# Cutting the first 8 MB load of a streaming row-sum kernel into an even-partition and an odd-partition load

## The chip, the cores and the metric

The kernel runs on one core of a Trainium2 chip. The metric is the device time of one execution in microseconds. The core has separate engines that run side by side and meet only at semaphores: VectorE (DVE in the profile), ScalarE (ACT), GpSimd (POOL), TensorE (PE, unused here) and SyncE (SP), which issues the transfers. The transfers themselves are moved by 16 DMA engines, each of which works through its own queue of packets in order.

## The reference

The input is float32 of shape 32 x 512 x 1024, so 16,384 rows of 1,024 numbers, 67.1 MB. Each row is clamped at zero and summed:

```python
relu_x = np.maximum(x, 0)
return np.sum(relu_x, axis=-1).astype(np.float32)
```

The output is 16,384 sums, 64 KB. Nearly all of the traffic is reading the input once.

## The kernel before, in words

The chip's memory for tiles (SBUF) has 128 partitions. The kernel gives each partition 128 rows in all: 16 rows from the first 2,048 rows of the input (`xf`), and 112 rows from the rest (`xv`). It goes through them in blocks of `ROWS = 16` rows per partition, which is 128 x 64 KB = 8 MB. There are `NB = 7` full blocks, and an eighth one that comes in smaller loads at the end (8 rows, 4 rows, then four pieces cut out of the last 4 rows). In the first block, partition p takes rows 16p to 16p+15, so the whole block is one contiguous 8 MB of the input, 64 KB of it per partition.

Three buffers `io0` to `io2` of 8 MB take the blocks in turn. The loads are all issued by SyncE in program order, through `load` (line 97, the transfer at line 99). Each load has its own semaphore from `sems.loads`, and adds 16 to it once all of it has landed. The first three loads wait for nothing. From the fourth on, a load waits on SyncE until VectorE has finished with the buffer it overwrites (line 101).

ScalarE clamps a block in place (`clamp`, lines 115 to 124) and VectorE sums its rows (`total`, lines 126 to 131). The lists `TWO`, `ACT` and `DVE` (lines 14 to 16) say how the rows of a block are cut: the first three blocks are clamped by one instruction each, later ones by two. The last rows go singly, some clamped and summed by ScalarE alone (`act_row`), some by VectorE alone (`dve_row`). ScalarE's very first instruction is the load of its function table, and that one carries the wait for the first block (line 118); the first clamp follows it without a wait of its own.

The order on SyncE is the order of the calls. Nothing schedules it anew, with one exception: `open_without_barrier` (line 241) takes the first `EARLY` instructions of SyncE (line 24, one before the change) out of the body and puts them into the program's opening block, ahead of everything else that SyncE does there. So the first load is SyncE's first instruction, then comes a branch to the body, then the second and third loads.

At the end SyncE issues three small stores: the sums of the first block, nearly all other sums, and the last two columns.

Of the kernel before, what the change touches and what calls it, by code (L numbers as in the profile page):

```python
# [5 lines left out]
RELU = mybir.ActivationFunctionType.Relu  # L6
# [3 lines left out]
ROWS = 16  # L10
NBUF = 3
# [9 lines left out]
START_PIECE, END_PIECE = 280, 260  # L21
PIECES = [240, 244]

EARLY = 1


def kernel(tc: tile.TileContext, x: bass.AP, out: bass.AP):
    nc = tc.nc
    sems = Semaphores(tc)

    tc.close()
    tc.compile()
    nc.cur_bb = nc.bb_map[tc.start_bb_name]
    body = nc.cur_bb.bb.instructions
    ends = list(body)
    body.clear()
    n_stores = relu_sum(nc, sems, x, out)
    body.extend(ends)


    nc.cur_bb = nc.bb_map[tc.start_bb_name + "_end"]
    nc.cur_bb.bb.instructions.clear()
    nums = sorted(s.num for s in (*sems.loads, sems.act, sems.dve))
    cleared = range(nums[0], nums[-1] + 1)
    assert len(cleared) == len(nums)
    nc.sync.sem_clear(cleared)
    nc.sync.wait_ge(sems.stored, 16 * n_stores).then_inc(sems.stored, -16 * n_stores)
    open_without_barrier(tc, EARLY)

# [10 lines left out]
def relu_sum(nc, sems: Semaphores, x: bass.AP, out: bass.AP):  # L60
# [24 lines left out]
    def rows(m, n):  # L85
        if m < ROWS:
            return xf[:, m : m + n, :]
        return xv[:, m - ROWS : m - ROWS + n, :]
# [5 lines left out]

    n_load = n_act = n_dve = n_store = 0

    def load(dst, src, after=None):
        nonlocal n_load
        dma = nc.sync.dma_start(out=dst, in_=src)  # L99
        if after:  # L100
            dma.wait_op(sems.dve, after[1], "sem-ge")
        dma.then_inc(sems.loads[n_load], 16)
        n_load += 1
        return sems.loads[n_load - 1]
# [10 lines left out]
    def clamp(ap, loaded):  # L115
        nonlocal n_act
        if n_act == 0:
            nc.scalar.preload_act_table(RELU).wait_op(loaded, 16, "sem-ge")  # L118
            loaded = None
        i = nc.scalar.activation(out=ap, in_=ap, func=RELU)  # L120
        if loaded is not None:
            i.wait_op(loaded, 16, "sem-ge")
        i.then_inc(sems.act, 1)
        n_act += 1

    def total(ap, m, n):
        nonlocal n_dve
        nc.vector.tensor_reduce(  # L128
            out=res[:, m : m + n], in_=ap, axis=mybir.AxisListType.X, op=ADD
        ).wait_op(sems.act, n_act, "sem-ge").then_inc(sems.dve, 1)  # L130
        n_dve += 1

    def act_row(ap, accum_out, loaded):
        nonlocal n_act
        i = nc.scalar.activation(out=ap, in_=ap, func=RELU, accum_out=accum_out)  # L135
        if loaded is not None:
            i.wait_op(loaded, 16, "sem-ge")
        i.then_inc(sems.act, 1)
        n_act += 1

    def dve_row(ap, accum_out, loaded):
        nonlocal n_dve
        i = nc.vector.tensor_scalar(  # L143
            out=ap,
            in0=ap,
            scalar1=0.0,
            scalar2=None,
            op0=MAX,
            op1=ADD,
            accum_out=accum_out,  # L150
        )
        if loaded is not None:
            i.wait_op(loaded, 16, "sem-ge")
        i.then_inc(sems.dve, 1)
        n_dve += 1

    freed = []
    m = 0
    for j in range(NB):
        buf = bufs[j % NBUF]  # L160
        loaded = load(buf[:, :, :], rows(m, ROWS), j >= NBUF and freed[j - NBUF])
        c = 0
        act_waits = dve_waits = loaded
        for n in TWO[j]:
            clamp(buf[:, c : c + n, :], act_waits)
            total(buf[:, c : c + n, :], m + c, n)
            act_waits = None
            c += n
        for _ in range(ACT[j]):
            act_row(buf[:, c, :], res[:, m + c : m + c + 1], act_waits)  # L170
            act_waits = None
            c += 1
        for _ in range(DVE[j]):
            dve_row(buf[:, c, :], res[:, m + c : m + c + 1], dve_waits)
            dve_waits = None
            c += 1
        assert c == ROWS
        freed.append((n_act, n_dve))
        m += ROWS


    buf = bufs[NB % NBUF]
    c = 0
    for n in TAIL:
        loaded = load(
            buf[:, c : c + n, :], rows(m, n), None if c else freed[NB - NBUF]
        )
        for i in range(n):
            if i % 2 == 0 or (n == 8 and i == 7):
                act_row(buf[:, c, :], res[:, m : m + 1], loaded if i == 0 else None)  # L190
            else:
                dve_row(buf[:, c, :], res[:, m : m + 1], loaded if i == 1 else None)
            c += 1
            m += 1

    flat = buf[:, :, :].rearrange("p c d -> p (c d)")
    src = rows(m, 4).rearrange("p c d -> p (c d)")
# [4 lines left out]
    last, w = parts[-1], PIECES[-1]  # L202
    others = [last[:, w + i : w + i + 1] for i in range(extra)]
    loaded = load(flat[:, at : at + b], src[:, :b])
    act_row(buf[:, c, :], res[:, m : m + 1], loaded)
    sums_act = n_act
# [3 lines left out]
    loaded = load(flat[:, at + end : at + 4 * D], src[:, end:])  # L210
# [30 lines left out]
def open_without_barrier(tc: tile.TileContext, n_loads: int):  # L241

    SP = mybir.EngineType.SP
    blocks = tc.nc.main_func.blocks
    opening = blocks[0].instructions
    body = next(b for b in blocks if b.name == tc.start_bb_name).instructions
    for i in list(opening):
        if isinstance(i, (mybir.InstDrain, mybir.InstEventSemaphore)):  # L250
            opening.remove(i)
    loads = [i for i in body if i.engine == SP][:n_loads]
    for i in loads:
        assert isinstance(i, mybir.InstDMACopy)
        body.remove(i)
    at = next(n for n, i in enumerate(opening) if i.engine == SP)
    opening[at:at] = loads
# [30 lines left out]
```

## Time and profile before

| | us |
|---|---|
| median of 3 runs | 160.94 (160.88 to 161.14) |
| span of the profiled execution | 159.8 |
| the runs' median over that span | 1.1 |
| VectorE busy | 117.6 |
| ScalarE busy | 104.2 |
| GpSimd busy | 0.2 |

The span runs from the first to the last instruction that the profile records, and it begins with SyncE's first load. The time of a run covers also what lies around the span; the profile does not carry the profiled execution's own time as a run, so it is taken as the span and the 1.1 us by which the median stands over it. An engine's idle time is put down to what released it. "SPq" stands for SyncE's queue of transfers, and an issue there is only the time that SyncE needs to start a transfer, not the transfer. Besides the engine rows, the trace has one record per DMA packet; a packet of a full block is one partition's 64 KB.

### The profile page before, as it was taken

The page shows a single profiled execution, that of the slowest core. Times are in us where ns is not written, and L with a number is a line of the kernel's source. Part 1 is how long each engine was busy: PE and PEld are TensorE (multiplying, and loading weights), DVE is VectorE, ACT ScalarE, POOL GpSimd, SP SyncE. Part 2 cuts the span into 40 slices and gives each one's busy share as a digit, 9 for nine tenths or more (in the row PEclk, how much of TensorE's full clock was granted, in tenths as well). Part 3 has the DMA queues.
Part 4 walks back from the last instruction along what each step waited for, and adds up shares of the span by engine and source line. Part 5 has one row for each costly group of instructions (what it writes and reads, how often), then busy time and mean ns, then how long its engine had stood idle before and what let it go on. Part 6 is the DMA issues. An engine that isn't in the chain of part 4 may idle for free.

```text
span 159.8 us, 120 instructions
## 1 busy us (share of the span) xinstructions
DVE 117.6 (74%) x43; ACT 104.2 (65%) x50; POOL 0.2 (0%) x4
## 2 busy tenths in 40 slices
DVE  0000000006999799994999999999999999999986
ACT  0000049993699808996099951999329993499994
POOL 0000000000000000000000000000000000000000
DMA  8996996996996997999989969969969969898993
GB/s 279 508 508 279 525 508 279 525 492 295 525 492 295 525 459 328 525 394 394 525 361 426 525 295 492 525 262 525 508 279 525 508 279 525 377 410 385 425 416 102
DMA packets 2304, 67.18 MB, mean 420 GB/s; under 512 B 640, under 2 KB 896, under 8 KB 1024
## 3 DMA queue, kind: packets, MB, share of 16 engines
q1 hardware_dynamic: 2304, 67.18, 97.9%
HBM read 67.11 MB, written 0.07 MB: 420 GB/s over the span
## 4 chain that ended last, share of the span: by engine, by line
DMA 44%; DVE 33%; ACT 17%; another core or an unknown queue 3%; SPq 1%; issue 0%
DMA io<-in_x_dram 44%; DVE res L128 32%; ACT io L120 17%; SPq L99 1%; DVE io L143 0%; DVE piece L227 0%; DVE piece L143 0%
## 5 line engine op out<-in xcount | busy, mean ns | idle before, releaser
L128 DVE TENSOR_REDUCE res<-io 128x8 f32<-128x8192 f32 (+2 forms) x9 | 101.1, 11286 | 40.2 <-ACT io L120 40.2
L120 ACT ACTIVATE io<-io 128x8192 f32<-128x8192 f32 (+2 forms) x9 | 81.7, 9111 | 26.0 <-DMA io<-in_x_dram 25.9
L135 ACT ACTIVATE io<-io 128x1024 f32<-128x1024 f32 x20 | 20.9, 1044 | 6.1 <-DMA io<-in_x_dram 6.1
L143 DVE TENSOR_SCALAR_CACHE_REDUCE io<-io 128x1024 f32<-128x1024 f32 (+2 forms) x15 | 15.8, 1110 | 0.6 <-DMA io<-in_x_dram 0.4
L118 ACT ACT_TABLE_LOAD x1 | 1.3, 1283 | 22.0 <-DMA io<-in_x_dram 22.0
L135 ACT ACTIVATION_READ_ACCUMULATOR io<-io 128x1 f32 x20 | 3.7, 187 | 0.0
L143 DVE DVE_READ_ACCUMULATOR io<-io 128x1 f32 x15 | 1.2, 82 | 0.0
L227 DVE TENSOR_SCALAR_CACHE_REDUCE piece<-piece 128x247 f32<-128x247 f32 x1 | 0.4, 410 | 0.0
L143 DVE TENSOR_SCALAR_CACHE_REDUCE piece<-piece 128x240 f32<-128x240 f32 x1 | 0.4, 398 | 0.0
L272 POOL MEMSET const-bfloat16-1.0<- 128x1 bf16 x1 | 0.1, 102 | 0.0
L272 POOL MEMSET const-uint8-127<- 128x1 uint8 x1 | 0.1, 102 | 0.0
L272 POOL MEMSET const-float32-1.0<- 128x1 f32 x1 | 0.1, 99 | 0.0
L272 POOL MEMSET const-float32-0.0<- 128x1 f32 x1 | 0.1, 98 | 0.2 <-issue 0.2
L143 DVE DVE_READ_ACCUMULATOR piece<-piece 128x1 f32 x1 | 0.1, 84 | 0.0
L227 DVE DVE_READ_ACCUMULATOR piece<-piece 128x1 f32 x1 | 0.1, 83 | 0.0
## 6 DMA issues: line engine op xcount, KB each, us to landing
io<-in_x_dram SPq DMA_DIRECT2D x1, 4096.0 KB, 21.6
io<-in_x_dram SPq DMA_DIRECT2D x1, 2048.0 KB, 26.1
io<-in_x_dram SPq DMA_DIRECT2D x1, 1164.0 KB, 28.4
io<-in_x_dram SPq DMA_DIRECT2D x1, 642.0 KB, 29.6
piece<-in_x_dram SPq DMA_DIRECT2D x1, 122.0 KB, 29.2
piece<-in_x_dram SPq DMA_DIRECT2D x1, 120.0 KB, 29.4
io<-in_x_dram SPq DMA_DIRECT2D x7, 26.9
out_dram<-res SPq DMA_DIRECT2D x1, 55.0 KB, 1.6
```

What stands on the lines that cost most here:

```text
L99: dma = nc.sync.dma_start(out=dst, in_=src)
L118: nc.scalar.preload_act_table(RELU).wait_op(loaded, 16, "sem-ge")
L120: i = nc.scalar.activation(out=ap, in_=ap, func=RELU)
L128: nc.vector.tensor_reduce(out=res[:, m : m + n], in_=ap, axis=mybir.AxisListType.X, op=ADD).wait_op(sems.act, n_act, "sem-ge").then_inc(se ...
L135: i = nc.scalar.activation(out=ap, in_=ap, func=RELU, accum_out=accum_out)
L143: i = nc.vector.tensor_scalar(out=ap, in0=ap, scalar1=0.0, scalar2=None, op0=MAX, op1=ADD, accum_out=accum_out,)
L227: nc.vector.tensor_scalar(out=last[:, :], in0=last[:, :], scalar1=0.0, scalar2=None, op0=MAX, op1=ADD, accum_out=res[:, NT - 2 : NT - 1],) ...
L272: nc = _bacc.Bacc("TRN2", target_bir_lowering=False, num_devices=1)
```

## The change

The first block's load is made as two loads of 64 partitions each: first partitions 0, 2, 4 and so on to 126, then partitions 1, 3, 5 to 127. Both read the rows that belong to these partitions, and both add 16 to the same semaphore, the one that the single load had (`same` takes the counter of semaphores back by one). ScalarE's first instruction therefore waits for 32. `EARLY` becomes 2, so that both halves stand in the opening block, ahead of SyncE's branch. All later loads, and all instructions of the other engines, are as they were. Line numbers below line 98 shift by one to five.

```diff
-EARLY = 1
+EARLY = 2
...
-    def load(dst, src, after=None):
+    def load(dst, src, after=None, same=False):
         nonlocal n_load
+        n_load -= same
         dma = nc.sync.dma_start(out=dst, in_=src)
...
         if n_act == 0:
-            nc.scalar.preload_act_table(RELU).wait_op(loaded, 16, "sem-ge")
+            nc.scalar.preload_act_table(RELU).wait_op(loaded, 32, "sem-ge")
             loaded = None
...
-        loaded = load(buf[:, :, :], rows(m, ROWS), j >= NBUF and freed[j - NBUF])
+        if j == 0:
+            for k in range(2):
+                loaded = load(buf[k::2, :, :], rows(m, ROWS)[k::2], None, k == 1)
+        else:
+            loaded = load(buf[:, :, :], rows(m, ROWS), j >= NBUF and freed[j - NBUF])
```

## The prediction

> **What bounds the kernel now.** I read the page's first three parts first, to see which resource is full.
>
> ```profile
> span 159.8 us, 120 instructions
> DVE 117.6 (74%) x43; ACT 104.2 (65%) x50; POOL 0.2 (0%) x4
> DMA packets 2304, 67.18 MB, mean 420 GB/s; under 512 B 640, under 2 KB 896, under 8 KB 1024
> q1 hardware_dynamic: 2304, 67.18, 97.9%
> ```
>
> The reader is to see that neither compute engine is full, while the 16 DMA engines are, for 97.9% of the span. I then asked for busy times by stretches that run from the landing of one block to that of the next. The columns are the stretch, its length, the busy times of VectorE, ScalarE and GpSimd, a clock that has no meaning here, the DMA engines' share and what they moved.
>
> ```profile
> 0.00:1.00 1.00, 0.00 (x0) 0.00 (x0) 0.20 (x4) 1.00 0.00 0
> 4.50:21.50 17.00, 0.00 (x0) 0.00 (x0) 0.00 (x0) 1.00 1.01 436
> 22.05:41.37 19.32, 4.14 (x1) 15.14 (x3) 0.00 (x0) 1.00 1.00 434
> 41.37:60.72 19.35, 18.55 (x2) 13.86 (x2) 0.00 (x0) 1.00 1.00 434
> 60.72:80.06 19.34, 17.21 (x2) 13.85 (x1) 0.00 (x0) 1.00 1.00 434
> 80.06:99.42 19.36, 19.36 (x2) 13.95 (x2) 0.00 (x0) 1.00 1.00 433
> ```
>
> Every block takes 19.3 us to come in, at 434 GB/s, with no gap between blocks. Divided by 16 that is 27.1 GB/s per DMA engine, so a 64 KB packet takes 2.42 us, and eight of them, an engine's part of a block, 19.34 us. The packet records say the same: after an engine's first packet, nearly every one of the 896 takes 2.418 to 2.48 us. The next packet follows at once, and the record by which an engine ends a load takes 9 ns.
>
> Next I read the list of waits and the timeline, for what a late first block would meet.
>
> ```profile
> ACT io L120 <- DMA io<-in_x_dram: 25.9, 5, 5.5
> ACT L118 <- DMA io<-in_x_dram: 22.0, 1, 22.0
> SPq L99 <- DVE res L128: 123.5, 5, 53.1
> 0.00 54.81 SPq L99 DMA_DIRECT2D io<-in_x_dram  x4
> 37.23 17.22 DVE L128 TENSOR_REDUCE res<-io 128x16 f32<-128x16384 f32 x1 [37.23 <-ACT io L120]
> 60.72 13.86 ACT L120 ACTIVATE io<-io 128x16384 f32<-128x16384 f32 x1 [5.49 <-DMA io<-in_x_dram]
> ```
>
> ScalarE waits 22.0 us for the first block, and 4 to 5.5 us before each following one: it is always ahead of the transfers. The fourth load has to wait for the sum of the first block, which ends at 37.23 + 17.22 = 54.45 us; it is issued by 54.81, and the third block lands at 60.7. So the queue never runs dry, with 5.9 us to spare. Last, the chain that ended last:
>
> ```profile
> 0.43 40.91 DMA io<-in_x_dram
> 127.56 29.58 DMA io<-in_x_dram
> 157.17 0.43 DVE io L143 x2
> 157.96 0.42 DVE piece L227 x2
> ```
>
> It begins and ends with transfers; after the last landing at 157.15 only about 1.2 us of compute and the last store remain. Thus the end is the start of the stream, plus 64 packets' worth of time per engine, plus a short tail. Whatever the first block loses or gains in the DMA engines moves the end by the same amount.
>
> **The change part by part.** *Issue.* SyncE issues one more transfer. Its issues of block loads take 0.33 to 0.44 us each. The extra one lies beside 9 us or more of queued packets and costs nothing; the second and third block loads pass behind it, and the second is not needed until about 21 us. Without that cover the price would be 0.44 us. The branch is passed by one more load, and it does no work.
>
> *Semaphore.* ScalarE's table load waits for 32 instead of 16, that is for both halves, so it waits for the same bytes as before; it wakes when the last packet has landed. Behind it stand all clamps on ScalarE, and VectorE's sums wait for these. One more end record per engine is 9 ns. I cost both at nothing.
>
> *The start.* The first packets of the 16 engines begin between 1.01 and 1.91 us, and end between 3.99 and 4.78; from there each engine runs at its even pace, and the slowest of them, which began at 1.35 and took 3.43 for its first packet, stays the last to land in the following blocks. If a load of half as many rows is ready sooner, or sets the engines off more evenly, the end follows the slowest: at best the 0.79 us between the last and the first of these ends. At worst the same spread comes once more behind the second load, also 0.79. No later load shows any such spread anew, so I take zero.
>
> *The 64-partition loads.* This is the term that decides. Every block load in this trace writes 128 neighbouring partitions, and in that form 16 engines each have a way into SBUF at 27.1 GB/s. No load here writes every other partition. The favourable end: each half is dealt to 16 engines, four packets each, none in another's way. Then 4 x 2.418 = 9.67 us per half, 19.34 for both, and the term is zero. The unfavourable end: the 64 rows are dealt so that at any time two engines write through the same way, or only half of the engines get work. Then half of the 434 GB/s remains, 8.39 MB / 217 GB/s = 38.7 us, and the term is +19.34 us. A gain is excluded here, beyond the start's, since the engines are already at 100% in every stretch. Which value? The only rows near are the full loads, and they stand for the zero; but they have just what the change takes away, all 128 partitions in one load, so the distance from them is the whole question. [...] No row shows how the rows of a load are dealt to the engines. I suppose, without a row for it, that they are dealt by their count and not by the partitions' addresses; then an engine's four rows lie spread over twice as many partitions as in the full form, its way into SBUF need no longer be its own, and engines meet. I hold that for likelier, and take the upper end.
>
> [...] The row is the 434 GB/s with 128 partitions. [...] No run here shows a 64-partition load.
>
> *Sum.* If two engines always meet, the first block's packets take 38.7 us instead of 19.34. The engines begin up to 0.9 us apart, so a pair does not meet all the time; I take off 0.3 us. First landing: 22.05 + 19.34 - 0.3 = 41.1 us. Then 13.86 of clamp after 1.28 of table load and 17.22 of sum follow as before, the fourth load is issued at about 73.9, and the third block lands at about 79.7: the 5.9 us to spare stay. So the whole stream moves by 19.0: 159.8 + 1.1 + 19.0 = 179.9, or 160.94 + 19.0 = 179.9 from the median.
>
> **The rivals.** *No collision, nothing else* (chance 0.20). The halves take 9.67 us each and the time is 160.94 within 0.1. For it speaks that every load in this trace runs at 434 GB/s, also those with a row pitch in the input of 448 KB instead of the first block's 64 KB; so the 128 KB step in the input costs nothing by itself.
>
> *No collision and an earlier or more even start* (0.15). This is the case on the other side: half the rows are ready sooner, or the slowest engine's 4.78 us draws nearer to the middle of the others, about 4.3. Price: 0.3 to 0.5 us, so about 160.5; it decides if the 64-row loads are dealt without collision and the slowest engine gains over 0.32 us. Against it: SyncE's issue of the small piece loads, 0.45 us each, is no shorter than that of the 8 MB loads, so the rows' count, 128 in all of them, may or may not set it.
>
> *Partial collision* (0.11). Only some engines meet, or pairs run out of step and use the idle way part of the time. Between the two ends: an extra quarter to a half of 19.34, or 5 to 10 us, 166 to 171.
>
> *A second slow start* (0.04). The odd half begins as the first packets did, with part of the 0.79 us spread again: 161.3 to 161.7.
>
> **How the numbers follow.** Full collision keeps 0.50, and its own range is 177 to 181. About 0.2%, 0.32 us, is what a measurement of this kernel can tell from no change, so same is 160.62 to 161.26. Slower is 0.50 + 0.11 + 0.04 = 0.65, same 0.20, faster 0.15. The range has to reach to both ends, since the cases without collision hold 0.35: from 160.5, which leaves out a part of the earlier start, to 181.0, the full 19.34 us and a slow start with it. Some 0.1 is left out.
>
> **What would show it.** In the changed kernel's timeline ScalarE's table load should stand at about 41 us instead of 22.05, and the stretch before it should move some 217 GB/s instead of 434, with packets of about 4.8 us; the stretches between later landings should still be 19.3 us. If the table load stands at 22 and the rate is 434, the dealing goes by partition and the forecast is wrong at that one term. If it stands at 21.6 or less, the start was the matter. If the first block is late and the end is not, my reading that the stream sets the end is wrong.

## The result and the profile after

The changed kernel takes 161.43 us (median, 161.28 to 161.61) against 161.00 us (160.88 to 161.31) for the kernel before. The ratio is 1.0023, with a 95% interval of 1.0015 to 1.0030. The change costs about 0.4 us. My forecast was 179.9 us. The time lies within the range I gave, in the lower part of it that I had kept for the cases without a collision; the forecast's main term, 19 us, did not come at all.

The page of the changed kernel, its first three parts:

```profile
span 159.9 us, 121 instructions
DVE 117.6 (74%) x43; ACT 104.2 (65%) x50; POOL 0.2 (0%) x4
DMA packets 2320, 67.18 MB, mean 420 GB/s; under 512 B 656, under 2 KB 912, under 8 KB 1040
q1 hardware_dynamic: 2320, 67.18, 97.9%
```

The reader is to see how little differs: 16 packets more (2320 against 2304, all of them in the count under 512 B, 656 against 640), which are the 16 engines' end records of the added load, and the same 97.9%. The stretches of the changed kernel, with the columns as in the prediction:

```profile
4.50:21.50 17.00, 0.00 (x0) 0.00 (x0) 0.00 (x0) 1.00 1.02 443
22.05:41.37 19.32, 4.07 (x1) 15.14 (x2) 0.00 (x0) 1.00 1.00 434
41.37:60.72 19.35, 18.50 (x2) 13.86 (x1) 0.00 (x0) 1.00 1.00 434
```

The first block comes in at the full rate. Its packets take 2.42 us (median), as before. The waits and the timeline:

```profile
ACT L119 <- DMA io<-in_x_dram: 22.1, 1, 22.1
SPq L100 <- DVE res L129: 122.6, 5, 52.1
...
22.12 1.28 ACT L119 ACT_TABLE_LOAD   x1 [22.12 <-DMA io<-in_x_dram]
41.48 13.86 ACT L121 ACTIVATE io<-io 128x16384 f32<-128x16384 f32 x1 [4.21 <-DMA io<-in_x_dram]
60.84 13.86 ACT L121 ACTIVATE io<-io 128x16384 f32<-128x16384 f32 x1 [5.49 <-DMA io<-in_x_dram]
```

ScalarE's table load stands at 22.12 us, not at 41. The landing of the first block and the next three come 0.07 to 0.12 us after those of the kernel before. That is all these two profiles show of a loss that the runs' times put at 0.4 us. What differs plainly is the beginning of the chain that ended last:

```profile
0.00 0.55 SPq L100
0.55 0.06 issue
0.61 0.58 SPq L100
1.19 0.04 issue
1.23 40.23 DMA io<-in_x_dram
```

SyncE's first issue takes 0.55 us; in the kernel before it took 0.38. By the packet records, the engines' first packets begin between 1.34 and 1.75 us instead of 1.01 and 1.91. The middle one of their ends moves from 4.30 to 4.63 us. The last of their ends, which sets the landings, moves only from 4.78 to 4.84.

### The profile page after: what moved, and what is told of

The parts are those of the page before. It is cut to its first block, busy times and chain, and to the rows that moved or that the text cites. A ratio compares the mean times of both kernels' runs of the same rounds, so it can differ in the third digit from the quotient of the medians.

```text
span 159.9 us, 121 instructions
## 1 busy us (share of the span) xinstructions
DVE 117.6 (74%) x43; ACT 104.2 (65%) x50; POOL 0.2 (0%) x4
## 2 busy tenths in 40 slices
DMA packets 2320, 67.18 MB, mean 420 GB/s; under 512 B 656, under 2 KB 912, under 8 KB 1040
## 3 DMA queue, kind: packets, MB, share of 16 engines
q1 hardware_dynamic: 2320, 67.18, 97.9%
## 4 chain that ended last, share of the span: by engine, by line
DMA 43%; DVE 34%; ACT 17%; another core or an unknown queue 3%; SPq 1%; issue 0%
DMA io<-in_x_dram 43%; DVE res L129 32%; ACT io L121 17%; DVE io L144 1%; SPq L100 1%; DVE piece L232 0%; DVE piece L144 0%
```

## The experiments

Two questions were open: where the 0.4 us comes from, and why the 19 us did not. For the first I held the theory "form": a load of every other partition takes SyncE longer to issue and its packets start later, and this is paid only where nothing else is in the queue, at the very start. (That it is the number of partitions and not the step of two came out only with the halves.) Its rivals were "crowding" (the second load right behind the first slows it), and a cost outside the recorded span.

### The kernel before, again

No edit.

> The kernel before, once more, to see how much of the 0.43 us lies in its span. Theory 'late start' (the changed kernel loses because its first packets begin 0.3 us later, and the profiled run of the kernel before had one unusually late DMA engine, so that its span hid this): 161.0 us, run spans near 159.6 to 159.7 us, that is 1.35 us under the time as in the changed kernel, and a last first-packet end near 4.4 to 4.5 us instead of 4.78. Rival 'outside the span' (the change costs time before or after the recorded span): spans near 159.8 to 159.9 us, only 1.1 us under the time.

Measured: 160.99 us, ratio to the kernel before 0.9998 (0.9989 to 1.0007). The spans of its runs, which are given to 0.1 us, lie 1.29 to 1.39 us under their times, and those of the changed kernel 1.31 to 1.40 (161.28 with a span of 159.9, 161.61 with 160.3). The profiled run has this chain at its start:

```profile
0.00 0.38 SPq L99
0.38 0.05 issue
0.43 40.80 DMA io<-in_x_dram
```

The last end of a first packet is 4.64 us, above the 4.4 to 4.5 that I expected, and the span is 159.7. The runs of the changed kernel have spans of 159.9 to 160.3, those of the kernel before mostly 159.5 to 159.8. So the loss lies within the span. The profile I forecast from was simply one of the longer runs of its kernel, with one engine that ended its first packet 0.2 us behind all the others, and the changed kernel's profile is that of its fastest run of twelve; beside each other they made the loss look smaller than it is. The ends of the 16 engines' last 64 KB packets tell it better than the last of them: their mean is 137.24 us in both profiles of the kernel before and 137.58 in the changed one, 0.34 us later.

### Only the even load ahead of the branch

```diff
-EARLY = 2
+EARLY = 1
```

> Even and odd load as in the changed kernel, but only the even one stands ahead of SyncE's branch. Theory 'form' (a load of every other partition is slow to issue and to start, whatever stands behind it): first issue again 0.55 us, first packets from 1.34 us, 161.4 us. Rival 'crowding' (the second load issued 0.06 us behind the first one slows the first one's start): with the branch between them the first issue falls back towards 0.38 us, first packets from 1.0 us, 161.0 to 161.1 us.

Measured: 161.45 us, ratio 1.0023 (1.0013 to 1.0034), the loss of the changed kernel. The branch between the two loads makes no difference to the issues: the first takes 0.55 us, the second begins at 0.60.

```profile
0.00 0.55 SPq L100
0.55 0.06 issue
0.60 0.58 SPq L100
```

So this run left the second load as close behind as it was, and what it rules out is that the hoisting past the branch costs the time; "crowding" needed the other runs.

### Two loads by rows instead of partitions

```diff
-                loaded = load(buf[k::2, :, :], rows(m, ROWS)[k::2], None, k == 1)
+                loaded = load(buf[:, 8 * k : 8 * k + 8, :], rows(m + 8 * k, 8), None, k == 1)
```

> The first block in two loads of all 128 partitions with 8 rows each (32 KB packets), both ahead of the branch and on one semaphore. Theory 'form': nothing of the loss, first issue 0.38 us, first packets from 1.0 us, 161.0 us. Rival 'crowding': the loss of the changed kernel, first issue 0.55 us, 161.4 us.

Measured: 160.94 us, ratio 0.9998 (0.9989 to 1.0006): no loss. Its chain begins:

```profile
0.00 0.38 SPq L100
0.38 0.05 issue
0.43 0.42 SPq L100
0.86 0.04 issue
0.90 40.36 DMA io<-in_x_dram
```

Two loads back to back in the opening block, half the bytes in each, one semaphore, a wait for 32: all that the change did, except that each load has 128 partitions. The issue is back at 0.38 us. This decides against crowding. The stretch from 1.00 to 1.35 us says the same; the last column counts a packet whole in the stretch where it begins, so it tells how many have begun. First the kernel before (its second profile), then the changed kernel, then the split by rows:

```profile
1.00:1.35 0.35, 0.00 (x0) 0.00 (x0) 0.00 (x0) 1.00 6.19 2060
```

```profile
1.00:1.35 0.35, 0.00 (x0) 0.00 (x0) 0.00 (x0) 1.00 1.11 374
```

```profile
1.00:1.35 0.35, 0.00 (x0) 0.00 (x0) 0.00 (x0) 1.00 4.14 1123
```

2060 GB/s for 0.35 us are 11 packets of 64 KB, 374 are 2, and 1123 are 12 of the 32 KB packets that the split by rows has. In the kernel before, 11 of the 16 engines are at work by 1.35 us; in the changed one two.

### The pair on the second block

```diff
-EARLY = 2
+EARLY = 1
...
-            nc.scalar.preload_act_table(RELU).wait_op(loaded, 32, "sem-ge")
+            nc.scalar.preload_act_table(RELU).wait_op(loaded, 16, "sem-ge")
...
-            i.wait_op(loaded, 16, "sem-ge")
+            i.wait_op(loaded, 32 if n_act == 1 else 16, "sem-ge")
...
-        if j == 0:
+        if j == 1:
```

> The first block in one load as in the kernel before; the second block in an even and an odd load instead. Theory 'form, paid only at the start': the 64-partition issues still take about 0.55 us, but beside 19 us of queued packets, so 161.0 us as before. Rival 'the packets of a 64-partition load cost more wherever it stands': 161.3 us or more.

Measured: 161.11 us, ratio 1.0004 (0.9995 to 1.0012). The pair's issues take 0.53 and 0.62 us, but they stand beside the queued first block:

```profile
0.00 0.37 SPq L100
0.37 0.05 issue
0.42 0.53 SPq L100
```

The packets of the pair cost nothing extra: the second block lands 19.32 us after the first (21.95 and 41.27 us). The loss is the start's alone.

### A small full load ahead of the pair

```diff
+            loaded = load(buf[:, :1, :], rows(m, 1))
             for k in range(2):
-                loaded = load(buf[k::2, :, :], rows(m, ROWS)[k::2], None, k == 1)
+                loaded = load(buf[k::2, 1:, :], rows(m + 1, ROWS - 1)[k::2], None, True)
```

`EARLY` is 3 here, and the table load waits for 48.

> A small load of all 128 partitions first (row 0, 4 KB packets, 0.5 MB, 1.2 us of transfer), then the even and the odd load of the other 15 rows of the block, all three on one semaphore and ahead of the branch. Theory 'form': the first issue falls to 0.38 us, first packets from 1.0 us, and the small load covers most of the slow issue behind it: 161.0 us, at most 161.2. Rival 'crowding' or 'more loads in the opening block cost time': 161.4 us or more.

Measured: 161.12 us, ratio 1.0006 (0.9997 to 1.0015). The chain begins:

```profile
0.00 0.37 SPq L100
0.37 0.05 issue
0.42 0.54 SPq L100
0.96 0.04 issue
1.01 0.59 SPq L100
```

Half a megabyte in front is cover enough for a slow issue, and three loads in the opening block do no harm by themselves. The interval leaves room for a rest of up to 0.2 us.

### Four loads of every fourth partition

```diff
-            for k in range(2):
-                loaded = load(buf[k::2, :, :], rows(m, ROWS)[k::2], None, k == 1)
+            for k in range(4):
+                loaded = load(buf[k::4, :, :], rows(m, ROWS)[k::4], None, k > 0)
```

`EARLY` is 4, and the wait is for 64.

> The first block in four loads of every fourth partition (32 each), all ahead of the branch. If what matters to the packets is that a load's partitions are spread evenly over all 128, they take 2.42 us and the first landing stays near 22 us; if rows are dealt in plain runs by count, two to an engine, engines meet and packets go towards 4.8 us, first landing near 41 us. Theory 'form' for the start: first issue 0.55 us or so again, 161.4 us; if a smaller count of partitions is slower still, more.

Measured: 161.44 us, ratio 1.0026 (1.0015 to 1.0036). First issue 0.55 us, first packets from 1.34 us, packets of 2.42 us. The first landing is at 22.24 us, and the rate is the full one:

```profile
0.00 0.55 SPq L100
...
4.50:21.50 17.00, 0.00 (x0) 0.00 (x0) 0.00 (x0) 1.00 1.05 455
```

Thirty-two partitions start as late as 64 (1.34 us in both), and two more loads cost nothing more (161.44 us against 161.43): the price here belongs to the first load alone, and it is no greater for 32 partitions than for 64.

### Halves instead of even and odd

```diff
-                loaded = load(buf[k::2, :, :], rows(m, ROWS)[k::2], None, k == 1)
+                loaded = load(buf[64 * k : 64 * k + 64, :, :], rows(m, ROWS)[64 * k : 64 * k + 64], None, k == 1)
```

> The first block in two loads of partitions 0 to 63 and 64 to 127 instead of even and odd. If rows are dealt to engines by count, and two engines on one way into SBUF halve each other, as my forecast supposed for the even and odd form: packets of 4.84 us in the first block, first landing at about 41 us, 179 to 180 us. If rows are dealt by the partition's place, so that each half goes to eight engines with eight packets each: packets of 2.42 us, first landing at about 22 us, 161.0 to 161.5 us.

Measured: 182.22 us, ratio 1.1317 (1.1301 to 1.1332). Its stretches and its timeline:

```profile
4.50:21.50 17.00, 0.00 (x0) 0.00 (x0) 0.00 (x0) 1.00 0.96 197
```

```profile
43.17 1.28 ACT L119 ACT_TABLE_LOAD   x1 [43.17 <-DMA io<-in_x_dram]
```

All 16 engines are at work, at a share of 0.96, and together they move 197 GB/s. A 64 KB packet takes 5.12 us (median) instead of 2.42, a factor of 2.12. This is the loss that I forecast, a little dearer than a plain halving, and it came where I had not put it. All 16 first packets begin between 1.35 and 1.76 us, and the first half's load ends with 16 counts between 22.37 and 22.96 us; so a load of 64 partitions is dealt to 16 engines, not to eight.

### Even and odd within each half

```diff
-            for k in range(2):
-                loaded = load(buf[k::2, :, :], rows(m, ROWS)[k::2], None, k == 1)
+            for k, s in enumerate((0, 1, 64, 65)):
+                loaded = load(buf[s : s + 63 : 2, :, :], rows(m, ROWS)[s : s + 63 : 2], None, k > 0)
```

`EARLY` is 4, and the wait is for 64.

> The first block in four loads of 32 partitions too, but even and odd within partitions 0 to 63, then even and odd within 64 to 127. If the ways into SBUF belong to fixed sets of partitions and those of one half are only eight, sixteen engines share eight ways as with the two halves: packets near 5.1 us, first landing near 42 us, about 182 us. If it is the stride of two that kept the engines apart, packets of 2.42 us and 161.4 us.

Measured: 182.40 us, ratio 1.1327 (1.1311 to 1.1342), with packets of 5.11 us:

```profile
4.50:21.50 17.00, 0.00 (x0) 0.00 (x0) 0.00 (x0) 1.00 0.98 200
...
ACT L119 <- DMA io<-in_x_dram: 43.5, 1, 43.5
```

A stride of two within one half does not keep the rate (200 GB/s); a stride of two or four over all 128 does (443 and 455 GB/s in the same stretch). In these runs what counts is whether the load in flight reaches both halves. Why that is so they do not show: a load of partitions 0 to 63 here also reads only the first 4 MB of the block, and no run confines the one without the other, so the limit may lie on the reading side or on the writing side. That the ways into SBUF belong to fixed sets of partitions was a supposition of mine; the 182 us that I worked out with it came, but no run shows such ways or how many there are.

All the runs together. "First issue" is SyncE's first transfer, "first packets" the earliest begin and the middle of the ends of the engines' first packets, all in us of the profiled run; with 4 KB or 32 KB first packets the ends do not compare and are left out.

| kernel | time, us | ratio (95%) | first issue | first packets: begin, middle end | 64 KB packet |
|---|---|---|---|---|---|
| before, again | 160.99 | 0.9998 (0.9989–1.0007) | 0.38 | 1.02, 4.29 | 2.42 |
| changed | 161.43 | 1.0023 (1.0015–1.0030) | 0.55 | 1.34, 4.63 | 2.42 |
| one load ahead of the branch | 161.45 | 1.0023 (1.0013–1.0034) | 0.55 | 1.33, 4.65 | 2.42 |
| two loads by rows | 160.94 | 0.9998 (0.9989–1.0006) | 0.38 | 1.02, – | 2.42 |
| pair on the second block | 161.11 | 1.0004 (0.9995–1.0012) | 0.37 | 1.01, 4.26 | 2.42 |
| small full load first | 161.12 | 1.0006 (0.9997–1.0015) | 0.37 | 1.01, – | 2.42 |
| every fourth partition | 161.44 | 1.0026 (1.0015–1.0036) | 0.55 | 1.34, 4.54 | 2.42 |
| halves | 182.22 | 1.1317 (1.1301–1.1332) | 0.56 | 1.35, 6.41 | 5.12 |
| even and odd in each half | 182.40 | 1.1327 (1.1311–1.1342) | 0.55 | 1.34, 6.30 | 5.11 |

No version is faster than the kernel before by more than its interval. The mean end of the engines' last 64 KB packets sorts the runs at the full rate in the same way: 137.24 us for the kernel before, 137.25 for the two loads by rows, 137.28 for the pair on the second block and 137.35 for the small load first, against 137.58 for the changed kernel, 137.60 for one load ahead of the branch and 137.56 for every fourth partition.

## Why the prediction was wrong

*The bound: right.* The transfers set the end. A later start of about 0.33 us came out as a loss of about 0.4, and a first block that was 21.1 us late (halves, table load at 43.17 instead of 22.05) as 21.2 us.

*The semaphore: right.* The last of the 32 counts comes at 22.11 us and the table load begins at 22.12.

*The 64-partition loads: this term failed.* I took the upper end, +19.34 less 0.3 us; it measured zero. The price was right in kind: confined to one half at a time, a block costs 21 us more, above my 19.34, since a packet takes 2.12 times as long and not twice. What failed is the supposition on how rows are dealt, for which I had no row: that a load of every other partition makes the engines meet on their way into SBUF. No run shows that term, neither a way that is an engine's own nor two engines that meet on one. The runs show in its place that a load spread evenly over all 128 partitions keeps the full rate, with packets of 2.42 us, at 64 or 32 partitions alike, and that one confined to a half does not (5.12 us, 197 to 200 GB/s). Nor does the half's loss come from engines without work: in the halves all 16 began at once, between 1.35 and 1.76 us. I had meant to read from a table load at 22 us and a rate of 434 GB/s that the dealing goes by partition; the changed kernel had 22.12 us and 443 GB/s, and that does not show it. The trace does not name a packet's engine, so which rows each one gets stays open.

*The issue and the start: the terms that I put at nothing, and that are the whole result.* In the issue's step I priced only the added transfer, rightly at nothing. I did not ask whether the first one's own issue would stay at 0.38 us, and took the rows of 128-partition loads for it; it takes 0.55. In the start's step I bounded the effect by 0.79 us either way and took zero; it is +0.33 in the begin and the middle end of the first packets, +0.34 in the mean end of the engines. The rival "a second slow start" named nearly the right size (161.3 to 161.7) for a wrong reason, at a chance of 0.04: it is the first start that is slower, and the odd half's packets follow the even half's without any new spread, at 2.418 to 2.422 us each. "Slower" was said and came true, but for another cause than the one it was said for.

*The yardstick.* I took 1.1 us to lie around the span, by setting a median beside one profile's span. In the runs that have both numbers it is 1.29 to 1.40 us; the profiled run was a long one, with a late engine. That does not spoil a forecast of 19 us, but for one of 0.4 the difference of 0.2 to 0.3 us is more than half of the effect.

What stays open: why a first load of 64 or 32 partitions takes 0.55 us to issue where one of 128 takes 0.38, although it has fewer rows. The longer issue is also only half of the later start: from its end to the first packet pass 0.79 us (0.55 to 1.34) instead of 0.63 (0.38 to 1.01), and no run tells what fills the other 0.16. The runs show that it goes with the number of partitions (which is here the number of a load's packets too), not with the bytes (the split by rows has the same bytes per load, and 0.38 us), not with the stride (the halves have none, and 0.56 us) and not with what stands behind it (in the split by rows a second load stands as close behind, from 0.43 us); they do not show what SyncE does in that time.

## What to carry to other kernels

Here the first transfer of the stream was the one whose issue time was bare: the pair cost 0.4 us there and nothing measurable on the second block (161.11 us). So give the first transfer the form that starts soonest, here all 128 partitions (an issue of 0.38 us against 0.55), and put unusual forms behind it, where half a megabyte of queued packets hid them in this kernel (161.12 us). If a load has to be split by partitions, try first the split in which each part is spread over all 128 (every second or fourth one, 2.42 us a packet here), not the one into the lower and the upper half, which more than halved the rate here (197 GB/s against 434) and cost 21 us on one 8 MB block. When a change may cost only some tenths of a microsecond, compare the mean over the DMA engines in two or more profiles, since the last engine of a single one can hide it: here the last of the first packets' ends moved by 0.06 us, the mean of the engines' last ends by 0.34.

## What the runs showed that I had not expected

- The first issue was slower with fewer partitions: 0.55 to 0.56 us for a first load of 64 or 32 partitions against 0.37 to 0.38 for 128, and the first packets begin 0.33 us later. The number of bytes made no difference at 128 partitions: 4 KB, 32 KB and 64 KB per partition all take 0.37 to 0.38.
- An issue's time also differed with what went before it. The full load right behind the pair takes 0.59 us in the changed kernel; in the split by rows, where it stands third too, it takes 0.43. The fourth issue, a full load again, takes 0.53 us in the changed kernel, but 0.55 in the split by rows, so that one is not the pair's doing. Beside queued packets no cost of this shows: the pair on the second block takes 161.11 us, ratio 1.0004 (0.9995 to 1.0012).
- Confined to one half of the partitions, the same packet took more than twice the time: 5.12 us against 2.42.
